# Expert rows loaded whole into three rooms, one comparison for both one-hots, sample rows left in PSUM

## The chip, the cores and the metric

One core of a Trainium2 chip runs the whole program. The metric is the device time of one execution in microseconds, lower is better. PE is TensorE, DVE VectorE, ACT ScalarE, POOL GpSimd and SP SyncE.

## What is computed

One decoder layer for a prompt group of 256 tokens and a sample group of 64 tokens: a mixer (state-space scan and short convolution), attention over 256 memory tokens, and PEER, a layer of 16384 single-neuron experts. The change lies in PEER. Its core, cut:

```
q = (xt @ wq).reshape(T, PEER_HEADS, 2, PEER_HALF)
s = einsum('thid,hikd->thik', q, sub_keys)
s1, i1 = top_k(s[:, :, 0], 16);  s2, i2 = top_k(s[:, :, 1], 16)
comb = s1[..., :, None] + s2[..., None, :]
sf, pos = top_k(comb, 16)            # 16 of 256 pairs in each of 8 heads
eid = i1 * 128 + i2 at pos;  g = softmax(sf)
act = gelu(einsum('td,tkd->tk', x, u[eid]))
out = einsum('tk,tkd->td', g * act, v[eid])
```

So every token takes 128 of the 16384 experts, each a row of 2048 numbers in `u` and one in `v` (128 MB each, as float32). All arithmetic is float32; matmuls run in a rounded format, so each operand is split into a high and a low part and each product takes three matmuls.

## The kernel before, in words

**Prompt tokens** are computed densely: for each of 128 blocks ("rows" in this text) of 128 experts the products of all 256 prompt tokens with all 128 experts are taken, and a gate matrix is laid over them that is zero where a token did not choose an expert. **Sample tokens** are gathered: for each of 64 places, 128 rows of `u` (1 MB) are fetched by an indirect transfer.

*Expert rows* (`u_unit(i, q)`, one call for a quarter q of row i, 512 units in all). Even quarters order half a row, 128 experts x 1024 columns, by four transfers into one 128x1024 tile `xt` (L1719, each to 32 partitions, in pieces of 256 numbers, 1 KB). DVE transposes 32x32 blocks (L1729, `tt`), ACT takes the high part (L1736, `H`), POOL or, when the planner finds POOL late, DVE the low part (L1739, L1742, `L`), and PE adds 12 matmuls to the row's sum `pu` (L1755 to L1757). After the fourth quarter ACT applies the Gelu (L1762, `at`) and SP stores the row of activations to DRAM (L1763).

*The order.* PE, ACT and DVE work in exactly the order in which the program issues instructions. The class `Stream` staggers each unit: its load is issued three units ahead of its first step, the second step one unit later, its matmuls six units after that. "Sides" (generators with a rate, so many steps for each unit) are woven in between: `choose` selects the experts, `sample_in` gathers and multiplies the sample rows, `gate_work` builds the gate matrices. SP and POOL queues keep their own in-order sequence of transfers.

*Rooms.* Weights, expert rows and value rows all take tiles of 128x1024 in turn from one ring of four (`wtile`, WB = 4).

*Sample products* (`sample_in`). The sample rows of x lie in SBUF (`XNAT`, copied from PSUM at L1488). For each place one DVE instruction multiplies the gathered 128x2048 tile `gu` with it and sums (L1612), and a second one reads the accumulator.

*Gates* (`one_hots`, `gates`). For four tokens at a time two one-hot matrices are made from the two key numbers of each choice (the key indices `n128p` lie in PSUM); the first is scaled by the gate. Normally DVE makes them, four comparisons with scaling of 128x128 (L1637) and one of 128x512 (L1645); when the planner finds ACT early enough, ACT makes the first kind (L1632, L1633). PE multiplies the two (L1661, `pgate`), ACT copies the result (L1674 to SBUF, L1671 to a tile that goes to DRAM). The tokens are in three parts, of 124, 76 and 56; the third part is kept in DRAM (`g2_d`) and read back in the value stage.

*Value stage* (`v_unit`). For each row the stored activations come back (L1844), POOL multiplies them by the three gate parts (L1852), ACT and DVE split the products and the value rows (L204, L205, `vt`), PE adds into eight PSUM banks, while sample values are gathered and added on DVE (L1805).

PSUM has eight banks, all handed out as tiles of 128x512 from one pool (`ps`).

## Time and profile before

| | us |
|---|---|
| median of the runs shown (3423.12, 3436.35, 3428.07) | 3428.07 |
| the profiled execution's own time | 3432.44 |
| its span, first to last instruction | 3430.7 |
| PE busy | 3212.5 |
| DVE busy | 2468.6 |
| ACT busy | 1580.3 |
| POOL busy | 1501.0 |

The expert rows' matmuls begin at 1721.8 us and end at about 2690; the value stage follows. A busy time is the union of an engine's instructions; the granted clock of PE is a share of its full 2.4 GHz, averaged over a stretch in which it is at one of its two levels, 1.2 and 2.4 GHz; the DMA share is the mean busy share of 16 engines.

### The profile page before, as it was taken

What the parts mean: (1) busy time and instruction counts of PE and PEld (TensorE: products, weight loads), DVE (VectorE), ACT (ScalarE), POOL (GpSimd) and SP (SyncE); (2) the same over time, 40 slices, a digit from 0 to 9 for tenths busy, and PEclk for the clock granted to TensorE, in tenths of its full rate; (3) what the DMA queues carried; (4) which work ended last, traced back from release to release, by engine and by line L of the source; (5) the groups of instructions that cost most, each with busy time, mean ns of one, the idle gap of its engine ahead of it and who ended that gap; (6) DMA issues with size and microseconds to landing.
All of it is one profiled execution on the core that took longest, in us unless ns stands there. A gap on an engine that the chain in (4) does not pass through costs nothing.

```text
span 3430.7 us, 60141 instructions
## 1 busy us (share of the span) xinstructions
PE 3212.5 (94%) x21357; PEld 3011.9 (88%) x21357; DVE 2468.6 (72%) x4393; ACT 1580.3 (46%) x3063; POOL 1501.0 (44%) x1555
## 2 busy tenths in 40 slices
PE   6999999999999998899999778888889999999997
PEld 6999999999999998799999778888889888878876
DVE  4556766666574577866777878898878588878875
ACT  4545543333553455554454344443334444444444
POOL 0001111111100002311288788887787677766753
PEclk8999999999999999999999999999999999999998
DMA  8664556555654587866887888999997999988986
GB/s 201 198 189 144 158 164 187 161 166 147 205 156 149 170 205 196 226 211 173 208 200 192 231 235 231 242 257 249 256 274 187 290 336 319 332 310 314 321 296 212
DMA packets 534922, 763.22 MB, mean 222 GB/s; under 512 B 46655, under 2 KB 447575, under 8 KB 525492
## 3 DMA queue, kind: packets, MB, share of 16 engines
q1 hardware_dynamic: 480060, 550.95, 56.2%
q0 software_dynamic: 54560, 208.44, 19.4%
q8 instruction: 167, 2.74, 0.3%
q14 instruction: 135, 1.11, 0.1%
HBM read 709.15 MB, written 49.80 MB: 221 GB/s over the span
## 4 chain that ended last, share of the span: by engine, by line
DMA 22%; PE 10%; issue 6%; DVE 6%; POOL 4%; SPq 2%; ACT 2%; DVEq 0%; POOLq 0%; ACTq 0%
DMA xt<-in_peer_u_dram 10%; DMA at<-act_d 6%; DMA gv<-in_peer_v_dram,EV 3%; PE pu L1757 2%; POOL L L1739 2%; PE pu L1755 2%; PE pu L1756 2%; DVE L L205 2%; DMA vt<-in_peer_v_dram 2%; POOL at L1852 2%; SPq L1719 2%; DVE tt L1729 1%; DVE slot L1805 1%; DMA act_d<-at 1%; DVE gu L1612 1%
## 5 line engine op out<-in xcount | busy, mean ns | idle before, releaser
L205 DVE TENSOR_TENSOR L<-W,H 128x512 fp32r<-128x512 f32 (+1 forms) x808 | 544.7, 701 | 291.9 <-ACT H L204 285.4
L1739 POOL TENSOR_TENSOR L<-tt,H 128x512 fp32r<-128x512 f32 x486 | 686.4, 1443 | 111.3 <-ACT H L1736 96.3
L1757 PE MATMUL pu<-XP,L 128*128 128x256 f32 x2048 | 599.9, 293 | 82.9 <-POOL L L1739 82.8
L204 ACT ACTIVATE H<-W 128x512 fp32r<-128x512 f32 (+1 forms) x808 | 476.0, 620 | 350.5 <-PE pg L287 241.8
L1755 PE MATMUL pu<-XP,H 128*128 128x256 f32 x2048 | 598.9, 292 | 18.7 <-ACT H L1736 12.4
L286 PE MATMUL pg<-AH,H 128*128 128x320 f32 (+1 forms) x1872 | 587.1, 314 | 3.9 <-ACT H L204 3.9
L1756 PE MATMUL pu<-XP,H 128*128 128x256 f32 x2048 | 590.3, 288 | 0.0
L288 PE MATMUL pg<-AH,L 128*128 128x320 f32 (+1 forms) x1872 | 578.7, 309 | 0.5 <-DVE L L205 0.5
L287 PE MATMUL pg<-AL,H 128*128 128x320 f32 (+1 forms) x1872 | 578.2, 309 | 0.0
L1736 ACT ACTIVATE H<-tt 128x512 fp32r<-128x512 f32 x512 | 316.6, 627 | 484.4 <-DVE tt L1729 411.2
L1757 PEld LDWEIGHTS pu<-XP,L 128*128 128x128 f32 x2048 | 404.3, 197 | 97.7 <-POOL L L1739 97.6
L1729 DVE STREAM_TRANSPOSE tt<-xt 128x512 f32<-128x512 f32 x512 | 341.3, 692 | 175.7 <-DMA xt<-in_peer_u_dram 155.3
L1755 PEld LDWEIGHTS pu<-XP,H 128*128 128x128 f32 x2048 | 405.2, 198 | 23.2 <-ACT H L1736 15.6
L1898 PE MATMUL acc<-L,wt 128*128 128x512 f32 x1024 | 402.5, 393 | 17.0 <-DVE L L205 16.5
L1756 PEld LDWEIGHTS pu<-XP,H 128*128 128x128 f32 x2048 | 404.4, 197 | 0.0
L1897 PE MATMUL acc<-H,wt 128*128 128x512 f32 x1024 | 400.4, 391 | 1.7 <-ACT H L204 1.7
L1899 PE MATMUL acc<-H,wt 128*128 128x512 f32 x1024 | 400.5, 391 | 0.0
L205 DVE TENSOR_TENSOR L<-vt,H 128x512 fp32r<-128x512 f32 x512 | 370.5, 763 | 36.6 <-ACT H L204 30.7
L286 PEld LDWEIGHTS pg<-AH,H 128*128 128x128 f32 (+1 forms) x1872 | 350.3, 187 | 9.0 <-ACT H L204 4.9
L204 ACT ACTIVATE H<-vt 128x512 fp32r<-128x512 f32 x512 | 292.1, 621 | 141.1 <-DMA vt<-in_peer_v_dram 91.8
L287 PEld LDWEIGHTS pg<-AL,H 128*128 128x128 f32 (+1 forms) x1872 | 350.4, 187 | 2.2
L288 PEld LDWEIGHTS pg<-AH,L 128*128 128x128 f32 (+1 forms) x1872 | 350.1, 187 | 1.9 <-DVE L L205 1.3
(491 smaller groups left out, 6157.6 us busy)
## 6 DMA issues: line engine op xcount, KB each, us to landing
xt<-in_peer_u_dram SPq DMA_DIRECT2D x1024, 128.0 KB
vt<-in_peer_v_dram SPq DMA_DIRECT2D x256, 512.0 KB
W<-in_w_in_dram SPq DMA_DIRECT2D x176, 512.0 KB
W<-in_w_out_dram SPq DMA_DIRECT2D x64, 512.0 KB
W<-in_w_mem_k_dram SPq DMA_DIRECT2D x32, 512.0 KB
W<-in_w_mem_v_dram SPq DMA_DIRECT2D x32, 512.0 KB
W<-in_w_mem_q_dram SPq DMA_DIRECT2D x32, 512.0 KB
kv<-in_cache_mem_k_dram SPq DMA_DIRECT2D x128, 128.0 KB
```

Of the source, the lines that this page charges most:

```text
L204: S.activation(h, src, AF.Copy)
L205: V.tensor_tensor(l, src, h.bitcast(F32), ALU.subtract)
L286: PE.matmul(out, hv[:, j, c0:c1], ah[:, k, 0:n], start=st, stop=False)
L287: PE.matmul(out, hv[:, j, c0:c1], al[:, k, 0:n], start=False, stop=False)
L288: PE.matmul(out, lv[:, j, c0:c1], ah[:, k, 0:n], start=False, stop=sp)
L1739: G.tensor_tensor(l, src, h.bitcast(F32), ALU.subtract)
L1755: PE.matmul(pu[:, 0:TP], hv[:, j], PP["xp"][:, 0, k], start=k == 0, stop=False)
L1756: PE.matmul(pu[:, 0:TP], hv[:, j], PP["xp"][:, 1, k], start=False, stop=False)
L1757: PE.matmul(pu[:, 0:TP], lv[:, j], PP["xp"][:, 0, k], start=False, stop=k == KC - 1)
L1897: PE.matmul(out, th, h, start=i == 0, stop=False)
L1898: PE.matmul(out, th, l, start=False, stop=False)
L1899: PE.matmul(out, tl, h, start=False, stop=i == P - 1)
```

## The change

1. **Rooms.** The ring becomes one tile of four rooms that the program hands out and takes back itself (`wtile`, `wtile2`, `wfree`); a pair of neighbouring rooms holds a whole row of 128x2048. When the selection begins, a third pair is added (`more`, from the smaller gate matrix: the parts of the tokens are now 108, 76 and 72). In the value stage the six rooms serve as halves.
2. **Row transfers.** A row is ordered at its first quarter by four transfers, each to 32 partitions as before but in pieces of 512 numbers, 2 KB, in the order 0, 2, 1, 3 of the partition groups. The layout of the prompt tokens' x in `xp` follows (columns 512 b + 128 ... for group b).
3. **Sample rows** stay in the four PSUM banks in which the transposition left them; each sample product becomes four instructions of 128x512 with accumulators in `DOT[..., 4]`, and one reduction at the end. As long as they live, no transposed quarter goes to PSUM.
4. **One-hots.** Both keys of four tokens in one DVE comparison of 128x1024; ACT scales the first by the gates, four times 128x128.
5. **Gates in DRAM.** The third part, now 72 tokens, is read back in four pieces into two halves of the slot in turn; the sample sum `ACC` moves to `GT`.
6. Small: `row`, `xs` and the key rows get tiles of their own or one room after the other.

The diff, cut:

```diff
-NG0, NG1 = 124, 76
+NG0, NG1 = 108, 76
 NG2 = TP - NG0 - NG1
-NGA = 8
+NGA = 6
...
-    def wtile(name="W"):
-        return wp.tile([P, 1024], F32, tag="W", bufs=WB, name=name)
+    wroom = cst.tile([P, 1024 * WB], F32, name="W")
+    rooms = [[wroom[:, 1024 * r:1024 * r + 1024], None, 0] for r in range(WB)]
+    turn = count(1)
+
+    def wtile(beside=None):
+
+        r = min((r for r in range(len(rooms)) if rooms[r][1] is None),
+                key=lambda r: (rooms[r ^ 1][1] is not beside, rooms[r][2]))
+        rooms[r][1] = rooms[r][0]
+        return rooms[r][0]
+
+    def wtile2():
+
+        r = min((r for r in range(0, len(rooms), 2) if rooms[r][1] is rooms[r + 1][1] is None),
+                key=lambda r: max(rooms[r][2], rooms[r + 1][2]))
+        w = (wroom if r < WB else more)[:, 1024 * (r % WB):1024 * (r % WB) + 2048]
+        rooms[r][1] = rooms[r + 1][1] = w
+        return w
...
     def key_rows():
-        kys = []
         for i in range(2):
-            kys.append(wtile("ky").rearrange("p (h c) -> p h c", c=P))
-            nc.sync.dma_start(kys[i], sub_keys[0, 4 * i:4 * i + 4].rearrange("h i k c -> k (h i) c"))
-        yield from wait(2)
...
+            ky = wtile()
+            nc.sync.dma_start(ky.rearrange("p (h c) -> p h c", c=P),
+                              sub_keys[0, 4 * i:4 * i + 4].rearrange("h i k c -> k (h i) c"))
+            yield from wait(2)
...
+        more = pL.tile([P, 2048], F32, name="W")
+        rooms.extend([more[:, 1024 * r:1024 * r + 1024], None, 0] for r in range(2))
...
-            S.activation(XNAT[:, 512 * q:512 * q + 512], pt, AF.Copy)
+            XNAT.append(pt)
...
                 gt = tiles.pop(j - AIN)
-                V.tensor_tensor_reduce(gt, gt, XNAT, 1.0, 0.0, ALU.mult, ALU.add, DOT[:, j - AIN:j - AIN + 1])
-                run("dve", 2.25, arrived.pop(j - AIN))
-            yield 1
-        S.activation(WS, DOT, AF.Gelu)
+                for q in range(4):
+                    part = gt[:, 512 * q:512 * q + 512]
+                    V.tensor_tensor_reduce(part, part, XNAT[q], 1.0, 0.0, ALU.mult, ALU.add, DOT[:, j - AIN, q:q + 1])
+                run("dve", 2.9, arrived.pop(j - AIN))
+            yield 1
+        XNAT.clear()
+        V.tensor_reduce(WS, DOT, AX.X, ALU.add)
+        S.activation(WS, WS, AF.Gelu)
...
-        by_act = [clock["act"] + A_MORE + 2 * i < clock["dve"] for i in range(2)]
+        at = run("dve", 1.3)
+        V.tensor_tensor(ov, PP["n128"].unsqueeze(1).unsqueeze(1).broadcast_to([P, 2, 4, P]),
+                        GT[:, 0:2, t0:t0 + 4].unsqueeze(3).broadcast_to([P, 2, 4, P]), ALU.is_equal)
+        yield ov, at
         for j in range(4):
...
-                at = run("dve", 0.26)
-                V.tensor_scalar(ov[:, 0, j], n128p, key(0), key(3), op0=ALU.is_equal, op1=ALU.mult)
...
+            S.activation(ov[:, 0, j], ov[:, 0, j], AF.Copy, scale=GT[:, 3, t0 + j:t0 + j + 1])
+            at = run("act", 0.3, at)
+            if j != 1:
+                yield ov, at
...
-            if q % 2 == 0:
-                xt = wtile("xt")
-                c0 = 512 * q
-                for b in range(4):
+            if q == 0:
+                xt = box["x", i] = wtile2()
+                for b in (0, 2, 1, 3):
                     nc.sync.dma_start(xt[32 * b:32 * b + 32].rearrange("p (a d) -> p a d", a=4),
-                                      U2[i * P:(i + 1) * P, c0 + 256 * b:c0 + 256 * b + 256].rearrange("(a p) d -> p a d", p=32))
-                box["x", i, q // 2] = xt
+                                      U2[i * P:(i + 1) * P, 512 * b:512 * b + 512].rearrange("(a p) d -> p a d", p=32))
...
-            tt = two("tt") if box["pool", n] else ps("tt")
+
+            tt = two("tt") if box["pool", n] or XNAT else ps("tt")
...
-        ACC = slot[:, 0:1024]
-        G2 = slot[:, 1024:1024 + P * NG2].rearrange("p (n x) -> p n x", x=4 * P)
+        ACC = GT.rearrange("p j t -> p (j t)")
+        G2 = [slot[:, 4096 * r:4096 * r + 32 * NG2].rearrange("p (n x) -> p n x", x=P) for r in range(2)]
...
-            if q == 1 and i in (4, 6, 8, 10):
-                r = i // 2 - 2
-                c0 = max(P * r, 4 * NGA)
-                nc.sync.dma_start(G2[:, :, c0:P * r + P], g2_d[:, :, c0:P * r + P])
+
+            if q == 1 and i in (2, 4, 36, 68):
+                r = (2, 4, 36, 68).index(i)
+                c0 = 4 * NGA if r == 0 else 0
+                nc.sync.dma_start(G2[r % 2][:, :, c0:], g2_d[:, :, P * r + c0:P * r + P])
```

How the instructions move, as the built programs have them. First SP, in the middle of the expert rows, with what each order waits for (DMAHW0 to 7 are the eight counters of its transfers, taken in turn, so each waits for the transfer eight places earlier; DVE for the room, Activation for the Gelu). Before, from one activation store to the next:

```order
L1763 DMA act_d<-at 128x256 [waits DMAHW3_49,Activation_49]
L1719 DMA xt<-in_peer_u_dram 32x4x256 [waits DMAHW4_49,DVE_49]
L1719 DMA xt<-in_peer_u_dram 32x4x256 [waits DMAHW5_49]
L1719 DMA xt<-in_peer_u_dram 32x4x256 [waits DMAHW6_49]
L1719 DMA xt<-in_peer_u_dram 32x4x256 [waits DMAHW7_49]
L1719 DMA xt<-in_peer_u_dram 32x4x256 [waits DMAHW0_49,DVE_49]
L1719 DMA xt<-in_peer_u_dram 32x4x256 [waits DMAHW1_49]
L1719 DMA xt<-in_peer_u_dram 32x4x256 [waits DMAHW2_49]
L1719 DMA xt<-in_peer_u_dram 32x4x256 [waits DMAHW3_49]
L1763 DMA act_d<-at 128x256 [waits DMAHW4_49,Activation_49]
```

and of the change:

```order
L1788 DMA act_d<-at 128x256 [waits DMAHW4_49,Activation_49]
L1743 DMA W<-in_peer_u_dram 32x4x512 [waits DMAHW5_49,DVE_49]
L1743 DMA W<-in_peer_u_dram 32x4x512 [waits DMAHW6_49]
L1743 DMA W<-in_peer_u_dram 32x4x512 [waits DMAHW7_49]
L1743 DMA W<-in_peer_u_dram 32x4x512 [waits DMAHW0_49]
L1788 DMA act_d<-at 128x256 [waits DMAHW1_49,Activation_49]
```

Between the stores of rows i and i+1 stood the second half of row i+3 and the first half of row i+4; now the whole of row i+4 stands there, in half as many orders. (Before the first store 28 orders, three and a half rows, stood there; now 16, four rows.)

Second DVE, where gathers and gates run beside the rows. Before:

```order
L1637 TENSOR_SCALAR oh<-n128p,GT 128x128
L1729 STREAM_TRANSPOSE tt<-xt 128x512
L1637 TENSOR_SCALAR oh<-n128p,GT 128x128
L1729 STREAM_TRANSPOSE tt<-xt 128x512
L1612 ISA gu,DOT<-gu,XNAT 128x2048
L1612 ISA DOT 128x1
L1729 STREAM_TRANSPOSE tt<-xt 128x512
L1637 TENSOR_SCALAR oh<-n128p,GT 128x128
L1645 TENSOR_TENSOR oh<-n128p,GT 128x512
```

and of the change:

```order
L1665 TENSOR_TENSOR oh<-n128p,GT 128x1024
L1752 STREAM_TRANSPOSE tt<-W 128x512 x3
L1648 ISA gu,DOT<-gu,pxn 128x512
L1648 ISA DOT 128x1
L1648 ISA gu,DOT<-gu,pxn 128x512
L1648 ISA DOT 128x1
L1648 ISA gu,DOT<-gu,pxn 128x512
L1648 ISA DOT 128x1
L1648 ISA gu,DOT<-gu,pxn 128x512
L1648 ISA DOT 128x1
L1752 STREAM_TRANSPOSE tt<-W 128x512 x2
```

The comparisons that lay between single transpositions are one instruction; a sample product is four pairs in a row at the same place.

Third ACT, where the gates are built. Before:

```order
L1762 ACTIVATE at<-pu 128x256
L1736 ACTIVATE H<-tt 128x512 x2
L1674 ACTIVATE G_23732<-pgate 128x128x4
L1736 ACTIVATE H<-tt 128x512 x2
L1762 ACTIVATE at<-pu 128x256
```

and of the change:

```order
L1787 ACTIVATE at<-pu 128x256
L1669 ACTIVATE oh<-oh,GT 128x128 x2
L1699 ACTIVATE G_23174<-pgate 128x128x4
L1761 ACTIVATE H<-tt 128x512
L1669 ACTIVATE oh<-oh,GT 128x128
L1761 ACTIVATE H<-tt 128x512 x3
L1787 ACTIVATE at<-pu 128x256
```

Between one row's Gelu and the next, four scalings have joined the high parts and the copy of a gate tile. DVE's program holds 27 low parts of its own (26 before); 24 of them read a quarter in SBUF.

## Rows read from the trace of the kernel before

**Rows 1.** The page's head: span, busy time of each engine.

```profile
span 3430.7 us, 60141 instructions
PE 3212.5 (94%) x21357; PEld 3011.9 (88%) x21357; DVE 2468.6 (72%) x4393; ACT 1580.3 (46%) x3063; POOL 1501.0 (44%) x1555
```

**Rows 2.** Busy time by stretches; after the engines the granted clock, DMA share, GB/s.

```profile
core 0: us, PE busy (x) PEld busy (x) DVE busy (x) ACT busy (x) POOL busy (x), PEclk, DMA share, GB/s
0.00:1711.00 1711.00, 1645.10 (x11513) 1592.58 (x11514) 1087.25 (x2219) 810.48 (x1578) 238.33 (x464) 0.99 0.63 181
...
1760.00:1810.00 50.00, 50.00 (x419) 50.00 (x418) 41.47 (x137) 24.96 (x47) 47.66 (x38) 1.00 0.91 211
1810.00:2610.00 800.00, 681.41 (x5278) 661.59 (x5277) 656.13 (x961) 335.08 (x650) 657.11 (x459) 0.95 0.91 241
2610.00:2660.00 50.00, 50.00 (x429) 50.00 (x428) 47.34 (x111) 25.04 (x48) 32.60 (x26) 1.00 0.62 153
...
2691.00:3431.00 740.00, 706.52 (x3072) 578.78 (x3072) 592.15 (x807) 346.24 (x670) 466.63 (x519) 0.98 0.89 307
```

**Rows 3.** Groups in 1810 to 2610: count, busy us, mean ns, idle before.

```profile
L1739 POOL TENSOR_TENSOR L<-tt,H 128x512 fp32r<-128x512 f32 x383 | 555.3, 1479 | 76.9 <-ACT H L1736 65.2 <-PE pu L1756 3.6 <-DVE tt L1729 3.2
...
L1729 DVE STREAM_TRANSPOSE tt<-xt 128x512 f32<-128x512 f32 x408 | 272.8, 693 | 135.9 <-DMA xt<-in_peer_u_dram 118.7 <-POOL L L1739 15.0 <-issue 1.8
...
L1612 DVE CUSTOM_DVE_ANT_0 gu<-gu,XNAT 128x2048 f32<-128x2048 f32 x64 | 232.6, 3635 | 0.0
...
L1637 DVE TENSOR_SCALAR oh<-n128p,GT 128x128 f32<-128x128 f32 x152 | 56.6, 375 | 0.0
...
L1645 DVE TENSOR_TENSOR oh<-n128p,GT 128x512 f32<-128x512 f32 x47 | 31.7, 674 | 0.0
L1633 ACT ACTIVATE oh<-oh,GT 128x128 f32<-128x128 f32 x40 | 19.8, 495 | 1.3
...
L1742 DVE TENSOR_TENSOR L<-tt,H 128x512 fp32r<-128x512 f32 x26 | 17.4, 669 | 5.1 <-ACT H L1736 5.1
...
L1612 DVE DVE_READ_ACCUMULATOR2_ANT DOT<- 128x1 f32 x64 | 5.0, 78 | 0.0
```

**Rows 4.** Who waited for whom in 1810 to 2610: us in total, times, longest.

```profile
ACT H L1736 <- DVE tt L1729: 366.9, 186, 8.1
DVE tt L1729 <- DMA xt<-in_peer_u_dram: 118.7, 65, 6.2
...
PE pu L1757 <- POOL L L1739: 82.8, 70, 6.3
POOL L L1739 <- ACT H L1736: 65.2, 55, 5.9
```

**Rows 5.** The chain of waits through 1810 to 2610, shares by line.

```profile
by line: DMA xt<-in_peer_u_dram 40.3%; issue 14.1%; POOL L L1739 8.9%; SPq L1719 6.7%; DVE tt L1729 5.4%; PE pu L1757 3.9%; PE pu L1756 3.4%; PE pu L1755 3.4%; DVE gu L1612 2.6%; ACT H L1736 2.0%; DMA act_d<-at 1.5%; POOL gu L1607 1.0%; DVE
```

**Rows 6.** What SP's queue waited for in 1810 to 2610: total, times, longest.

```profile
SPq L1763 <- ACT at L1762: 117.8, 68, 8.0
SPq L1719 <- DMA xt<-in_peer_u_dram: 101.4, 104, 4.1
```

**Rows 7.** The sample products L1612: ns least, median, most.

```profile
L1612 DVE CUSTOM_DVE_ANT_0 gu<-gu,XNAT x64: 2248/2794/8392, 1905.4 to 2593.4; 128x2048 f32<-128x2048 f32 x64
```

**Rows 8.** The group of POOL's subtractions in 1710 to 1850.

```profile
L1739 POOL TENSOR_TENSOR L<-tt,H 128x512 fp32r<-128x512 f32 x86 | 109.6, 1312 | 19.3 <-ACT H L1736 18.0 <-PE pu L1756 1.1
```

**Rows 9.** Short stretches: weights in 2 KB, in 1 KB; then three inside G.

```profile
1500.00:1540.00 40.00, 40.00 (x275) 40.00 (x274) 25.31 (x46) 20.27 (x39) 0.00 (x0) 1.00 0.58 192
1560.00:1600.00 40.00, 40.00 (x275) 39.83 (x274) 24.36 (x41) 17.84 (x34) 0.24 (x1) 1.00 0.42 132
...
1960.00:2010.00 50.00, 34.99 (x254) 33.84 (x253) 38.78 (x49) 17.61 (x32) 47.02 (x27) 0.86 0.77 206
2110.00:2160.00 50.00, 36.70 (x266) 35.72 (x265) 46.39 (x52) 25.17 (x55) 41.01 (x26) 0.83 0.72 187
2510.00:2560.00 50.00, 41.95 (x332) 40.12 (x331) 37.39 (x40) 18.11 (x34) 43.76 (x32) 1.00 1.03 277
```

More of the change, by code (lines that the diff above doesn't have):

```diff
@@ L184, in step, with wfree @@
     GAIN = cst.tile([P, 96], F32, name="GAIN")
-    def wtile(name="W"):
-        return wp.tile([P, 1024], F32, tag="W", bufs=WB, name=name)
+    wroom = cst.tile([P, 1024 * WB], F32, name="W")
[12 more added lines that the diff above has]
+        return w
+    def wfree(w):
+        for r in rooms:
+            if r[1] is w:
+                r[1:] = None, next(turn)
+    more = None
     def high():
@@ L252, in load @@
                 if kq in (0, 2) and w0 is not None:
-                    box["w"] = w0[kq // 2]
+                    box["room", kq + 1] = w0[kq // 2]
+                    box["w"] = w0[kq // 2].rearrange("p (k n) -> p k n", n=ncol)
                 elif kq % 2 == 0:
-                    w = wtile()
+                    w = box["room", kq + 1] = wtile(box["room", kq - 1] if kq % 4 else None)
                     wv = w[:, 0:4 * ncol].rearrange("p (k n) -> p k n", n=ncol)
@@ L267, in prep @@
                 split(hv, lv, box.pop(("w", kq))[:, 2 * q:2 * q + 2])
+                if q == 1:
+                    wfree(box.pop(("room", kq)))
                 box[kq] = (hv, lv)
@@ L361, in step @@
     mem = [tokens() for _ in range(2)]
-    w0 = [wtile().rearrange("p (k n) -> p k n", n=256) for _ in range(2)]
+    w0 = [wtile()]
+    w0.append(wtile(w0[0]))
     for i in range(2):
@@ L618, in put_columns @@
         for q in range(nchunk // 8):
-            row = wtile("row")[0:ncol]
+            row = pS.tile([P, 1024], F32, tag="row", bufs=1, name="row")[0:ncol]
             for g in range(2):
@@ L993, in load @@
                 if k % 2 == 0:
[L994 removed]
+                    box["room", k + 1] = wtile()
+                    w = box["room", k + 1].rearrange("p (k n) -> p k n", n=512)
                     nc.sync.dma_start(w, w2d[k * P:(k + 2) * P, 512 * c:512 * c + 512].rearrange("(k p) n -> p k n", p=P))
@@ L1006, in prep @@
                     split(h, l, src)
+                if k % 2:
+                    wfree(box.pop(("room", k)))
                 box[k] = h, l
@@ L1338, in open_p @@
         strm.side(norm_p(), 1)
-        strm.side(key_rows(), 0.5)
+        strm.side(key_rows(), 0.75)
         PP["normed"] = strm.side(normed(), 0.4)
@@ L1349, in key_rows @@
     def key_rows():
[L1350 removed]
         for i in range(2):
[L1352 to L1360 removed]
+            ky = wtile()
+            nc.sync.dma_start(ky.rearrange("p (h c) -> p h c", c=P),
+                              sub_keys[0, 4 * i:4 * i + 4].rearrange("h i k c -> k (h i) c"))
+            yield from wait(2)
+            for q in range(2):
+                pt = ps("pky")
+                for j in range(4):
+                    transpose(pt[:, j * P:(j + 1) * P], ky[:, 512 * q + P * j:512 * q + P * j + P])
+                S.activation(PP["KY"][:, 8 * i + 4 * q:8 * i + 4 * q + 4], pt.rearrange("p (j k) -> p j k", k=P), AF.Copy)
+                yield 1
+            wfree(ky)
         done.add(("ky",))
@@ L1386, in normed @@
                 if q % 2 == 0:
-                    xs = wtile("xs")[0:n]
+                    xs = pp.tile([P, 1024], F32, tag="xs", bufs=1, name="xs")[0:n]
                 pt = ps("pxs")
@@ L1457, in step @@
         gemm(w_peer_q[0], 256 * c, 256, BH, BL, T, lambda m, pt, c=c: evac_p(m, pt, c))
-    pL = pT = GT = EID = EV = GS = DOT = WS = XNAT = None
+    pL = pT = GT = EID = EV = GS = DOT = WS = None
+    XNAT = []
     def choice_in():
-        nonlocal pL, pT, GT, EID, EV, GS, DOT, WS, XNAT
+        nonlocal more, pL, pT, GT, EID, EV, GS, DOT, WS
         drain(PP["normed"])
@@ L1576, in choose @@
             if tb < 2:
+                yield from wait(2)
                 pt = ps("pgt")
```

47 lines of the change are left out of this document (14 added, 33 removed).

## The prediction, before the change was run

> **What bounds the kernel now.** I read the page first: the span is 3430.7 us and PE is busy for 3212.5 us of it [rows 1], so at most some 218 us are to be had from waits. The profiled execution's own time is 3432.44 us, 1.74 above its span; the median of the runs shown is 3428.07, so 4.37 us come off a time that is summed against the profiled execution. A difference under 0.5%, 17 us, can't be told from no change here.
>
> Then the busy time by stretches [rows 2]. PE is busy without a gap at 1760 to 1810 and at 2610 to 2660, at a granted clock of 1.00 (2.4 GHz). Between them, from 1810 to 2610 (stretch G), it is busy for 681.4 of 800 us at a mean granted clock of 0.95: 118.6 us of idle time. Of the two long stretches around it the first has 65.9 us of idle time in 1711 and the last, the expert values, 33.5 in 740. G is where the selection, the 64 gathers and most of the gate one-hots run beside the expert rows, and every row of the change that costs or saves more than a few us lies in it. 408 quarters of a row (a quarter is one transposition L1729, so G holds 102 of the 128 rows) are worked there [rows 3].
>
> Then the waits in G, from PE backwards [rows 4]. PE waits for POOL's low parts (82.8 us), POOL for ACT's high parts (65.2), ACT for DVE's transpositions (366.9), DVE for the expert rows in flight (118.7). The chain of waits in G names those transfers with 40.3% of the stretch, and the matmuls with some 11% [rows 5]. So the rows come late, and it is not one engine that is full: DVE 656, POOL 657, ACT 335 of 800 us, the DMA engines 0.91 [rows 2]. SyncE, which orders the transfers, itself waits 117.8 us for an activation behind which the next rows are queued, and 101.4 us for a transfer of eight places earlier to land [rows 6].
>
> **The change part by part.**
>
> *Sample products on DVE.* Before, 64 products of 128x2048 take 232.6 us and their 64 accumulator reads 5.0, 237.6 together [rows 3]. After, there are 256 of 128x512 with one operand in PSUM and 256 reads. The nearest row is the subtraction of the same size with a PSUM source, L1742, 669 ns; with a read of 78 ns [rows 3] one costs 747 ns, and 256 cost 191.2 us: 46.4 us less. Bounds: a quarter of the shortest old product, 2248/4 = 562 ns [rows 7], gives 163.8 us (73.8 less); a quarter of the mean, 3635/4 = 909 ns [rows 3], gives 252.7 us (15.1 more). The old product lies between 2248 and 8392 ns with the same operands [rows 7], and POOL's subtraction took 1312 ns before the first product [rows 8] and 1479 in G [rows 3]: each lengthens the other. I take 747 ns for that reason, and give POOL the difference back, 383 x (1479 - 1312) = 64 us of its busy time; at worst nothing.
>
> The Trainium skill, SBUF — State Buffer, section "SBUF: two separate sides", states for this that a VectorE instruction with two SBUF inputs shuts GpSimd's reads out for its whole length and the other way round, and that one with a single SBUF input does not. By it the new products run undisturbed, and DVE's gain is the 46 us or more; by the mean alone it would be a loss of 15. The spread of 2248 to 8392 ns agrees with the rule. It also speaks against one edit: while the products run, a quarter that DVE subtracts itself now has both inputs in SBUF.
>
> That last edit concerns 24 of 27 such quarters (26 before, all from PSUM). From 669 ns each they can grow by what a POOL subtraction lasts, 1479 ns [rows 3]: 0 to 35 us on DVE. I take 10.
>
> *One-hots on DVE and ACT.* Four tokens cost DVE up to 4 x 375 + 674 = 2174 ns. G holds 152 of the first kind and 47 of the second, 56.6 + 31.7 = 88.3 us [rows 3]. Now it is one comparison of 128x1024. The slope between 512 and 2048 elements, (2248 - 674)/1536 = 1.02 ns an element [rows 3, 7], makes it 674 + 524 = 1198 ns; 47 of them 56.3 us, 32 less (bounds: 2 x 674 = 1348 ns gives 25 less; 674 + 375 = 1049 ns gives 39 less). ACT takes over 256 scalings of 128x128; at the 495 ns of its nearest row [rows 3] they are 127 us at most, for 188 of them (47 groups) in G 93. In G it is busy for 335 of 800 us [rows 2], which covers this as long as nobody waits for a place in its queue; if that cover is gone, see the third rival.
>
> DVE's work in G so falls from 656 by 46 - 10 + 32 = 68 to 588 us, POOL's from 657 to 593.
>
> *Transfers.* 1024 orders of 128 KB in pieces of 1 KB become 512 of 256 KB in pieces of 2 KB. SyncE gives half as many orders, and eight that are under way are 2 MB instead of 1. By the rows of its order, what follows an activation's store was the second half of the row three ahead and the first of the row four ahead; now it is the whole row four ahead, so half a row more has been ordered at the same point. Three rooms hold 3 MB where four held 2. None of this removes the wait for the activation; it is a later row that is queued behind it. The last activations and the value loads behind them keep their order.
>
> The price of a piece isn't in the trace. Weights in pieces of 1 KB run at 132 GB/s with a share of 0.42, 314 GB/s if the engines were full; those in pieces of 2 KB at 192 and 0.58, 331 [rows 9]: 5% less time per byte. Expert rows alone, in 1 KB, run at 211 and 0.91, 232 full; at 153 and 0.62, 247 [rows 2]. With 247, the 408 quarters of 256 KB, 107 MB, hold 433 of the 728 us (0.91 of 800) that the engines are busy in G. Bounds: nothing saved; or the rows reach the weights' 331, 107/0.331 = 323 us, 110 less. I take a tenth, 43 us: twice the weights' ratio, because more is under way and neighbours in the queue go to different halves of the partitions, and far from 110, because each transfer still lands in 32 partitions, as the slow rows do. That leaves 685 us.
>
> *What G then lasts.* The transfers set it: before, 728 us of work took 800, a share of 0.91. At the same share 685 us take 753; at 0.94, with a deeper reserve, 729. The other floors are lower: PE's 681 us at 0.95 of the clock, between 647 and 681; DVE 588; POOL 593. I take 745 us: **55 us less**. Half of the 118.6 us of idle time goes; what is late next is still the row, then POOL's subtraction.
>
> *The rest.* The value stage gets six rooms instead of four, 1 MB more of gates to write and read back (3.4 us of transfers at its 307 GB/s [rows 2]) and gives its gates to POOL in parts of 108, 76 and 72 instead of 124, 76 and 56. With 33.5 us of idle time in it I take 0, between 10 less and 10 more. The first 1711 us hold the same transfers in the same order in the same four rooms; the key rows take one room after the other instead of two at once: 0, at most 3 either way. Four copies of the sample rows (now read where the transposition left them) and a reduction of 256 values are under 3 us, beside other work.
>
> Sum: 3432.4 - 55 = 3377 for a profiled execution, **3373 us** as a median.
>
> **The rivals.**
>
> *A: the rows can't come faster.* If 32 partitions are the limit, the pieces' size saves nothing. For it: the rows alone reach 0.91 at only 211 GB/s [rows 2], while weights over all partitions reach 314 [rows 9]. Against it: 277 GB/s ran in one 50 us stretch with the gathers [rows 9]. Then only the places gain where DVE was late and the transfers were not full, such as 1960 to 2010 and 2110 to 2160, shares of 0.77 and 0.72, 28 us of PE idle time together [rows 9]; of that some 17: 3411. The Trainium skill, SBUF — State Buffer, "Door 1: The DMA port swizzle", has this as a rule: 32 partitions reach 8 of 16 ports, about 218 GB/s at most, and two transfers to different halves at once bring 6% over one. By it G would keep its 728 us but for those 6% of 433, 26 us; the 211 GB/s agree, and no run here shows the order's part.
>
> *B: the rows cease to be the limit.* With 323 us for the rows G needs 618 us of transfers, 657 at 0.94, and PE's floor is at 647 to 681: some 680, 120 less, 3308. For it: all idle time lies in G. Against it: nothing shows 331 GB/s into 32 partitions.
>
> *C: PSUM takes it back.* While the products run, four of eight banks hold the sample rows and one the key indices; three are left for the rows' sums and the gates, where transpositions and sums had seven. In the built program 27 of 64 gate tiles take a bank whose sum ended only two to four quarters before, and 29 sums one that a gate tile left four to seven quarters before. Such a bank is free when ACT has read it, and in ACT's order that read stands behind the high parts of five further quarters. ACT waits for a transposition 186 times, 366.9 us in G [rows 4], 1.97 us each. If each of the 56 takings meets one such wait, PE stands still for 110 us; less the gain, 55 more than before: 3483. It decides from (55 + 17)/1.97, some 37 takings, on. Against it: two quarters are 2.9 us at PE's pace of 1.43 us (12 matmuls at 419 in 50 us [rows 2]), and with rows on time ACT is ahead.
>
> *D: no change that can be seen*, the gains of G given back in part by DVE's double-input quarters and by ACT's longer queue: 3424.
>
> **How the numbers follow.** Forecast 0.53, A 0.17, B 0.10, C 0.12, D 0.08. A lies at the 17 us bound, half of it either side. Faster: 0.53 + 0.10 + 0.08 = 0.71; within 0.5%: 0.09 + 0.08 = 0.17; slower: C, 0.12. The range takes in the forecast with its bounds, A, D and the nearer part of B: 3322 to 3430. Left out are C and the far end of B.
>
> **What would show it.** Right: in G (found again as the stretch between two gapless ones) idle time of PE near 60 us; DVE's waits for the rows well under 118 us; SyncE's wait for a landing under 50; products near 0.67 us with little spread and POOL's subtraction near 1.3 us. A: DMA share at 0.95 or more with the same GB/s and DVE still waiting for rows. C: PE waiting at a gate tile or at a row's first matmul for ACT's reads (at<-pu, G<-pgate), tens of times. The forecast is wrong if the stretch shortens by under 25 or by over 90 us, or if the value stage moves by over 10.

## The result and the profile after

The changed kernel takes 3388.19 us (median of 4 runs, 3382.60 to 3394.76), the kernel before beside it 3432.21 (3423.12 to 3446.70): a ratio of 0.987, 95% interval 0.984 to 0.990, 44 us less. 3373 was forecast, in a range of 3322 to 3430. The profiled execution is the longest of the four: 3394.76 us, span 3393.0.

The page's head, beside [rows 1]:

```profile
span 3393.0 us, 59499 instructions
PE 3210.2 (95%) x21357; PEld 3016.0 (89%) x21357; DVE 2373.0 (70%) x4563; ACT 1609.9 (47%) x3235; POOL 1421.2 (42%) x1554
```

DVE works 96 us less, POOL 80 less, ACT 30 more, PE nearly the same: what went is PE's idle time. The busy time by stretches, columns as in [rows 2]:

```profile
1760.00:1810.00 50.00, 50.00 (x419) 50.00 (x418) 43.61 (x147) 25.38 (x48) 45.62 (x37) 1.00 0.87 214
1810.00:2580.00 770.00, 686.52 (x5389) 669.31 (x5388) 587.76 (x1224) 365.77 (x782) 596.53 (x466) 0.96 0.93 254
2580.00:2630.00 50.00, 50.00 (x429) 50.00 (x428) 31.57 (x39) 39.06 (x103) 32.24 (x26) 1.00 0.68 164
```

G, between two gapless stretches, is now 1810 to 2580 us and holds 83.5 us of PE's idle time, where it held 118.6 [rows 2]. From the first expert-row matmul to the first value matmul it is 928.5 us (1731.8 to 2660.3), before 969.6 (1721.8 to 2691.4): 41 less. This is the row stage. The value stage behind it is 7 shorter. The row stage begins 10 later in this execution; in the ten experiments that keep the changed kernel's first part it begins between 1723.0 and 1728.0 (before: 1721.8), so most of the 10 is this execution's own.

The waits in the stretch, beside [rows 4] (total us, times, longest), all engines first, then the rest of PE's:

```profile
ACT H L1761 <- DVE tt L1752: 325.9, 171, 8.7
DVE tt L1752 <- DMA W<-in_peer_u_dram: 143.6, 51, 7.7
POOL L L1764 <- ACT H L1761: 128.8, 96, 5.9
PE pu L1782 <- POOL L L1764: 31.3, 35, 4.1
...
PE pu L1780 <- ACT H L1761: 12.2, 9, 2.9
PE pgate L1686 <- ACT at L1787: 10.2, 4, 4.5
PE pu L1780 <- ACT G L1699: 7.1, 3, 3.1
PE pu L1780 <- ACT g L1696: 6.1, 3, 2.7
PE pgate L1686 <- ACT g L1696: 5.1, 4, 3.0
PE pgate L1686 <- ACT G L1699: 3.7, 2, 2.5
PE pgt L220 <- ACT at L1787: 3.6, 1, 3.6
```

PE's wait for POOL fell from 82.8 to 31.3 us. New are waits until ACT has read a PSUM bank: the last six rows, and one of 0.8 us more, make 36.6 us in 18 waits. Two waits in the selection are gone that PE had before in 1810 to 2610 us:

```profile
PE pgt L197 <- DVE GA L1574: 15.9, 2, 8.3
```

There PE stood until DVE had the gates of a group of tokens ready (`GA`), which PE then transposes (`pgt`). The change has a line for this that its cut diff leaves out: `yield from wait(2)` lets the program put other work between the two. No run undoes that line alone.

VectorE's wait for rows has not fallen: 143.6 us where it was 118.7, in fewer waits but longer ones. VectorE works 68 us less in a stretch that is 30 us shorter, so it stands idle for longer in any case; this wait by itself doesn't tell how late the rows are. SyncE's waits, beside [rows 6]:

```profile
SPq L1788 <- ACT at L1787: 329.1, 81, 9.0
SPq L1788 <- ACT oh L1669: 66.4, 16, 8.2
SPq L1697 <- ACT g L1696: 41.3, 18, 5.1
SPq L1788 <- DMA W<-in_peer_u_dram: 24.4, 24, 4.3
SPq L1743 <- DMA W<-in_peer_u_dram: 11.8, 14, 1.8
SPq L1743 <- DVE tt L1752: 8.5, 22, 0.9
```

SyncE hardly waits for landings (101.4 us before) or rooms. It stands at the activation's store for over half the stretch, with the next row's order behind it. The groups, beside [rows 3, 8], and the products alone (ns min/median/max), beside [rows 7]:

```profile
L1648 DVE CUSTOM_DVE_ANT_0 gu<-gu,pxn 128x512 f32<-128x512 f32 x256 | 158.8, 674 | 0.0
L1665 DVE TENSOR_TENSOR oh<-n128p,GT 128x1024 f32<-128x1024 f32 x51 | 60.6, 1187 | 0.0
L1767 DVE TENSOR_TENSOR L<-tt,H 128x512 fp32r<-128x512 f32 x27 | 38.4, 1423 | 1.4 <-ACT H L1761 1.0 <-issue 0.3
L1648 DVE DVE_READ_ACCUMULATOR2_ANT DOT<- 128x1 f32 x256 | 20.9, 82 | 0.0
...
L1764 POOL TENSOR_TENSOR L<-tt,H 128x512 fp32r<-128x512 f32 x390 | 505.9, 1323 | 142.1 <-ACT H L1761 128.8 <-PE pu L1782 5.8 <-issue 1.8
```

```profile
L1648 DVE CUSTOM_DVE_ANT_0 gu<-gu,pxn x256: 641/681/687, 1906.9 to 2558.4; 128x512 f32<-128x512 f32 x128
```

### The profile page after: what moved, and what is told of

The parts are those of the page before. It is cut to its first block, busy times and chain, and to the rows that moved or that the text cites. A ratio compares the mean times of both kernels' runs of the same rounds, so it can differ in the third digit from the quotient of the medians.

```text
span 3393.0 us, 59499 instructions
## 1 busy us (share of the span) xinstructions
PE 3210.2 (95%) x21357; PEld 3016.0 (89%) x21357; DVE 2373.0 (70%) x4563; ACT 1609.9 (47%) x3235; POOL 1421.2 (42%) x1554
## 4 chain that ended last, share of the span: by engine, by line
DMA 18%; PE 14%; DVE 8%; issue 5%; POOL 3%; ACT 2%; SPq 1%; DVEq 0%; ACTq 0%; POOLq 0%
DMA W<-in_peer_u_dram 8%; DMA at<-act_d 6%; PE pu L1782 3%; PE pu L1780 3%; PE pu L1781 2%; DMA gv<-in_peer_v_dram,EV 2%; DVE tt L1752 2%; DVE L L228 2%; POOL at L1880 2%; DVE gu L1648 1%; PE acc L1929 1%; PE acc L1930 1%; PE acc L1928 1%; POOL L L1764 1%; SPq L1743 1%
## 5 line engine op out<-in xcount | busy, mean ns | idle before, releaser
L228 DVE TENSOR_TENSOR L<-W,H 128x512 fp32r<-128x512 f32 x1320 | 913.1, 724 | 324.2 <-ACT H L227 307.0
L227 ACT ACTIVATE H<-W 128x512 fp32r<-128x512 f32 x1320 | 762.2, 620 | 409.3 <-PE pg L313 246.0
L1764 POOL TENSOR_TENSOR L<-tt,H 128x512 fp32r<-128x512 f32 x485 | 626.3, 1318 | 171.5 <-ACT H L1761 150.6
L1782 PE MATMUL pu<-XP,L 128*128 128x256 f32 x2048 | 593.5, 290 | 32.9 <-POOL L L1764 31.3
L1752 DVE STREAM_TRANSPOSE tt<-W 128x512 f32<-128x512 f32 x512 | 332.0, 686 | 213.1 <-DMA W<-in_peer_u_dram 161.8
L1782 PEld LDWEIGHTS pu<-XP,L 128*128 128x128 f32 x2048 | 401.1, 196 | 42.5 <-POOL L L1764 40.7
L1880 POOL TENSOR_TENSOR at<-at,G 128x108 f32<-128x108 f32 (+1 forms) x256 | 209.3, 837 | 219.0 <-DMA at<-act_d 199.5
L1929 PEld LDWEIGHTS acc<-L,wt 128*128 128x128 f32 x1024 | 192.9, 188 | 58.5 <-DVE L L228 18.2
```

The costliest lines, as they stand in the source:

```text
L227: S.activation(h, src, AF.Copy)
L228: V.tensor_tensor(l, src, h.bitcast(F32), ALU.subtract)
L1764: G.tensor_tensor(l, src, h.bitcast(F32), ALU.subtract)
L1782: PE.matmul(pu[:, 0:TP], lv[:, j], PP["xp"][:, 0, k], start=False, stop=k == KC - 1)
L1929: PE.matmul(out, th, l, start=False, stop=False)
```

## Experiments

Twelve kernels, each beside the kernel before. The ratio is to the kernel before, with its 95% interval; the kernel before had a median of 3432 to 3437 us beside them, so a difference of under 5 us from the changed kernel tells nothing. "Longer" and "shorter" are against the changed kernel's 3388 us. The last column is the row stage in the profiled execution, from the first expert-row matmul to the first value matmul; it is 969.6 us in the kernel before.

| run | edit | us | ratio | row stage, us |
|---|---|---|---|---|
| changed kernel | | 3388 | 0.987 (0.984 to 0.990) | 928.5 |
| e1 | its order 0, 1, 2, 3 | 3415 | 0.994 (0.993 to 0.996) | 953.4 |
| e2 | 1 KB pieces | 3392 | 0.989 (0.986 to 0.991) | 926.6 |
| e3 | products against SBUF | 3414 | 0.993 (0.991 to 0.995) | 949.3 |
| e4 | old one-hots | 3390 | 0.986 (0.983 to 0.989) | 931.6 |
| e5 | transfers over 128 partitions | 4105 | 1.195 (1.192 to 1.197) | 1640.6 |
| e7 | two rooms | 3450 | 1.004 (1.003 to 1.006) | 978.0 |
| e8 | sums share banks | 3423 | 0.997 (0.995 to 0.999) | 970.5 |
| e9 | stores on ACT's queue | 3399 | 0.990 (0.987 to 0.993) | 927.5 |
| e10 | half rows | 3415 | 0.994 (0.993 to 0.996) | 959.3 |
| e12 | store one row later | 3370 | 0.982 (0.979 to 0.986) | 904.9 |
| e6 | before, order 0, 2, 1, 3 | 3415 | 0.995 (0.993 to 0.997) | 952.2 |
| e11 | before, that order and PSUM products | 3398 | 0.990 (0.987 to 0.994) | 941.0 |

**e1, the order alone.**

```diff
-                for b in (0, 2, 1, 3):
+                for b in range(4):
```

> The changed kernel with one line undone: each expert row's four transfers go out as 0, 1, 2, 3 and not as 0, 2, 1, 3. Theory one (the rows come sooner because the pieces are 2 KB and a row is whole, the order is worth nothing): 3388 us within 6 us of the changed kernel, TensorE's idle time between 1810 and 2580 us stays about 84 us. Rival (two neighbouring groups of 32 partitions fill through the same engines, and the swapped order is what spreads them): 15 to 40 us longer, 3403 to 3428 us, with DVE's waits for the rows in that stretch above 143.6 us.

3415 us, 27 longer: the rival. The stretch 1810 to 2580 and its wait for rows:

```profile
1810.00:2580.00 770.00, 677.59 (x5225) 658.76 (x5225) 567.31 (x1203) 350.32 (x742) 576.31 (x451) 0.94 0.97 249
```

```profile
DVE tt L1752 <- DMA W<-in_peer_u_dram: 175.2, 56, 8.9
```

Fewer bytes a second (249 for 254 GB/s) at a higher share (0.97 for 0.93): per byte the engines are busy 6% longer (0.97/249 against 0.93/254).

**e6, the order in the kernel before.** The same line there, the other way round.

> The kernel before with one line of the change: the four transfers of each half row go out as 0, 2, 1, 3 and not as 0, 1, 2, 3; 1 KB pieces, two double rooms, products and one-hots as before. Theory port (the order raises the rate into SBUF wherever rows are late): 10 to 25 us shorter than the kernel before, 3407 to 3422 us beside 3432. Rival (the order pays only once rows are whole and three are held, or once the products no longer hold GpSimd): within 6 us of 3432 us.

3415 us, some 20 less than the kernel before beside it (22 by the medians, 18 by the ratio). The same 770 us of this kernel, and of the kernel before:

```profile
1810.00:2580.00 770.00, 661.88 (x5166) 642.73 (x5164) 651.62 (x936) 327.70 (x637) 645.42 (x447) 0.95 0.86 247
```

```profile
1810.00:2580.00 770.00, 652.78 (x5042) 633.37 (x5041) 632.13 (x921) 320.61 (x623) 627.92 (x439) 0.95 0.91 242
```

0.86/247 against 0.91/242: 7% less engine time per byte, with 1 KB pieces and half rows. The order works by itself. The Trainium skill, SBUF — State Buffer, "Door 1: The DMA port swizzle", puts partitions 0 to 63 and 64 to 127 on different ports, and its section "Can I just issue two DMAs to hit both halves?" gives two transfers to different halves at once only 6% over one. Both pairs agree with the direction. That the sizes agree too is not shown: the 6 and 7% are of all bytes in the stretch, of which the rows are little more than half in the changed kernel (417 quarters of 256 KB, 109 of 196 MB), and e2 moves the share by 5% with no effect on the time.

**e2, the pieces alone.**

```diff
-                for b in (0, 2, 1, 3):
-                    nc.sync.dma_start(xt[32 * b:32 * b + 32].rearrange("p (a d) -> p a d", a=4),
-                                      U2[i * P:(i + 1) * P, 512 * b:512 * b + 512].rearrange("(a p) d -> p a d", p=32))
+                for h in range(2):
+                    for b in (0, 2, 1, 3):
+                        c0 = 512 * b + 256 * h
+                        nc.sync.dma_start(xt[32 * b:32 * b + 32].rearrange("p (a d) -> p a d", a=4)[:, :, 256 * h:256 * h + 256],
+                                          U2[i * P:(i + 1) * P, c0:c0 + 256].rearrange("(a p) d -> p a d", p=32))
```

> The changed kernel with each row's transfers halved: eight of 128 KB with 1 KB pieces in place of four of 256 KB with 2 KB pieces; rooms, order of the groups, products and one-hots stay as changed. Theory one (the piece size is worth the tenth that the prediction put on it, 43 us of the row transfers' 433 us in G): 25 to 45 us longer, 3413 to 3433 us, and the DMA share of the stretch at 1.00. Rival port (a row fills 32 partitions at a time at a rate that the piece size does not touch): within 6 us of 3388 us. [...]

3392 us: no difference that can be told. The pieces are worth nothing, and so is that more bytes are under way, since eight orders are half as many bytes here:

```profile
1810.00:2580.00 770.00, 688.56 (x5390) 672.69 (x5389) 584.81 (x1205) 369.29 (x793) 592.72 (x463) 0.95 0.88 254
```

The same 254 GB/s and the same work of PE, at a lower share. The share is not a fill: probably packets that wait in line count in it, and with orders of 128 KB instead of 256 KB fewer do. SyncE waits 121.3 us for landings again, and that costs nothing.

**e3, the products alone.** The sample rows are copied to SBUF as before, one product of 2048 columns a step.

```diff
-            XNAT.append(pt)
+            S.activation(XN["sb"][:, 512 * q:512 * q + 512], pt, AF.Copy)
...
-                for q in range(4):
-                    part = gt[:, 512 * q:512 * q + 512]
-                    V.tensor_tensor_reduce(part, part, XNAT[q], 1.0, 0.0, ALU.mult, ALU.add, DOT[:, j - AIN, q:q + 1])
+                V.tensor_tensor_reduce(gt, gt, XN["sb"], 1.0, 0.0, ALU.mult, ALU.add, DOT[:, j - AIN:j - AIN + 1])
```

> The changed kernel with the sample rows back in SBUF: one product of 2048 columns per sample step with both operands in SBUF, and four more PSUM banks free; rooms, transfers and one-hots stay as changed. Theory one (products that read PSUM relieve DVE and GpSimd): VectorE's products go from 179.7 us in 1810 to 2580 us to about 238 us, GpSimd's subtractions from 1.32 to about 1.5 us, and the kernel is 20 to 40 us longer, 3408 to 3428 us. Rival C (three banks take it back): the waits of matmuls on ScalarE's reads, about 36 us of TensorE's time, vanish and the kernel is 10 to 25 us shorter, 3363 to 3378 us. If both hold in equal measure, within 8 us of 3388 us, with the bank waits under 10 us and VectorE's and GpSimd's waits up by as much.

3414 us, 26 longer: theory one, though the banks' waits went as rival C has it. The product, POOL's subtraction, and PE's only waits of size:

```profile
L1647 DVE CUSTOM_DVE_ANT_0 gu<-gu,XNAT 128x2048 f32<-128x2048 f32 x64 | 247.6, 3869 | 0.1
...
L1761 POOL TENSOR_TENSOR L<-tt,H 128x512 fp32r<-128x512 f32 x370 | 547.9, 1510 | 63.3 <-ACT H L1758 54.3 <-issue 2.8 <-PE pu L1779 2.1
```

```profile
PE pu L1779 <- POOL L L1761: 90.6, 84, 7.0
PE pu L1777 <- ACT H L1758: 11.8, 14, 2.7
```

No wait for a bank is left, and PE's wait for POOL is back at 90.6 us. So the products against PSUM take away 59 us of waits for POOL (90.6 to 31.3) and bring 36.6 of waits for banks; what is left, 23, is about the 26 measured. VectorE's wait for rows is shorter here, 85.5 us, in a slower kernel.

**e4, the one-hots alone.** `one_hots` and the copy to GT as before.

```diff
-        at = run("dve", 1.3)
-        V.tensor_tensor(ov, PP["n128"].unsqueeze(1).unsqueeze(1).broadcast_to([P, 2, 4, P]),
-                        GT[:, 0:2, t0:t0 + 4].unsqueeze(3).broadcast_to([P, 2, 4, P]), ALU.is_equal)
+        by_act = [clock["act"] + A_MORE + 2 * i < clock["dve"] for i in range(2)]
...
```

> The changed kernel with the old one-hots: per four tokens one multiply-compare a token for the first key and one comparison for the second, some of both put on ScalarE, in place of one comparison of 1187 ns and four gate scalings of 392 ns. Theory one (VectorE's time matters only where a row has landed, and rows are late): VectorE works some 30 us more in 1810 to 2580 us, of which a third reaches TensorE, 5 to 15 us longer, 3393 to 3403 us. Rival (the scaling on ScalarE delays the high parts, and the old form is as good): within 5 us of 3388 us or up to 10 us shorter.

3390 us: DVE is busy 610.8 us in the stretch instead of 587.8, and no part of that can be told in the time. The one-hots are worth nothing.

**e7, the third room alone.**

```diff
-        more = pL.tile([P, 2048], F32, name="W")
-        rooms.extend([more[:, 1024 * r:1024 * r + 1024], None, 0] for r in range(2))
```

> The changed kernel without the third room: the rows whole in two rooms of 1 MB, the value stage in four rooms of 512 KB; all else as changed. Theory one (the third room lets a row be ordered while two are unread): 15 to 35 us longer, 3403 to 3423 us, with SyncE waiting for VectorE's transpositions before its row orders instead of for the activation. Rival (SyncE stands at the activation's store anyway, 329 us in 1810 to 2580 us, so that the third room is free long before the order comes): within 6 us of 3388 us.

3450 us, 61 longer: theory one's sign at twice its size, and 0.4% slower than the kernel before. Of the 61 some 50 lie in the row stage; the value stage, back in four rooms, has the rest. SyncE's two longest waits:

```profile
SPq L1741 <- DVE tt L1750: 219.2, 81, 8.3
SPq L1786 <- ACT at L1785: 207.9, 67, 7.0
```

A room of 1 MB comes free only when the whole row in it is transposed, and SyncE now stands before its row orders until then. Whole rows need the third room; without it they cost more than order and products give.

**e10, half rows in the six rooms.**

```diff
-            if q == 0:
-                xt = box["x", i] = wtile2()
+            if q % 2 == 0:
+                xt = box["x", i, q // 2] = wtile()
+                c0 = 512 * q
...
```

> The changed kernel with half rows again: each half row in one of the six rooms of 512 KB, four transfers of 128 KB in the order 0, 2, 1, 3, ordered half by half as in the kernel before; products, one-hots and the rest as changed. Theory one (what pays is the order, the products and half as much again of room; that a row is whole is worth nothing or costs, since its first transposition waits for all of it): 5 to 30 us shorter, 3358 to 3383 us. Rival (whole rows pay because a whole row is ordered at one place of SyncE's queue, ahead of the next store): 10 to 30 us longer, 3398 to 3418 us.

3415 us, 27 longer: the rival. VectorE's wait for rows:

```profile
DVE tt L1753 <- DMA W<-in_peer_u_dram: 182.9, 73, 7.5
```

It is not the pieces, since e2 has the same 1 KB in whole rows. What is left is that a row's second half is ordered two quarters later in the program, behind one store more, and into a room of its own; these were not taken apart.

**e11, order and products in the kernel before.** The edits of e6, and of e3 the other way round.

> The kernel before with two parts of the change: the order 0, 2, 1, 3, and the sample products in four pieces against PSUM; half rows in four rooms of 512 KB and the old one-hots stay. Theory one (these two parts are the whole gain, whole rows with the third room come to nothing together): the order's 20 and the products' 26 us add up, 3380 to 3396 us. Rival (the parts need the third room: with less in reserve the bank waits of three PSUM banks meet late rows): 3400 to 3430 us.

3398 us, between the two ranges: 34 of the 44 us come from these two parts, and the order's 20 leave 14 to the products there. All the rest of the change together, whole rows, third room, one-hots and the selection's `wait(2)`, is worth the other 10. PE's two waits at `pgt` are still there in e11, 12.4 us, so the `wait(2)` may be most of it; that is not shown. That e10, with two half rooms more, the new one-hots and the `wait(2)`, takes 17 us longer than e11 is not explained: the two also differ in how the tokens are cut (108, 76, 72 against 124, 76, 56) and in where the key rows lie.

**e5, transfers over all partitions.**

```diff
-                for b in (0, 2, 1, 3):
-                    nc.sync.dma_start(xt[32 * b:32 * b + 32].rearrange("p (a d) -> p a d", a=4),
-                                      U2[i * P:(i + 1) * P, 512 * b:512 * b + 512].rearrange("(a p) d -> p a d", p=32))
+                for a in range(4):
+                    nc.sync.dma_start(xt[:, 512 * a:512 * a + 512],
+                                      U2[i * P + 32 * a:i * P + 32 * a + 32].rearrange("p (b d) -> b p d", b=4))
```

> The changed kernel with each row's four transfers cut the other way: one transfer takes 32 experts whole and fills a 2 KB piece in each of the 128 partitions, in place of 128 experts' quarter into 32 partitions; same bytes, pieces, number of orders and same place of every value in SBUF. Theory port (how fast a row lands depends on which partitions the transfers under way fill; that is why the order 0, 2, 1, 3 is worth 27 us): the rows land sooner still, VectorE's waits for rows in 1810 to 2580 us fall from 143.6 to under 90 us and the kernel is 15 to 45 us shorter, 3343 to 3373 us. Rival (the order helped only by when the first half of a row is there, not by the rate): within 8 us of 3388 us. A third way: sixteen engines share each transfer in another way and the rate falls, over 3400 us.

4105 us: the third way, far beyond its bound. The queue's share between 1760 and 1900 us, and a row order on SyncE (ns min/median/max):

```profile
q1 hardware_dynamic: 8628, 15.17, 28.8%
```

```profile
L1743 SPq DMA_DIRECT2D W<-in_peer_u_dram x512: 522/2381/9178, 1701.6 to 3333.2; - x171
```

The share stands near a quarter while everything waits for rows, at 109 GB/s, and an order takes SyncE 2381 ns in the median instead of 430 in the changed kernel. A quarter fits four of sixteen engines, as many as the source has outer blocks here; the trace doesn't list the engines apart, so that is argued. What an even spread over the partitions would give stays open.

**e8, two sums in one bank.**

```diff
             if q == 0:
-                box["p"] = ps("pu")
+                if i % 2 == 0:
+                    box["pp"] = ps("pu")
+                box["p"] = box["pp"][:, TP * (i % 2):TP * (i % 2) + TP]
```

> The changed kernel with two expert rows' sums in the two halves of one PSUM bank, so that the sums take 64 banks in place of 128; all else as changed. Theory C (some 36 us of TensorE's idle time in 1810 to 2580 us are waits until ScalarE has read a bank): the waits of gate tiles and first matmuls of a row on ScalarE fall to under 12 us, half of what goes is met by a later wait for a row, 8 to 20 us shorter, 3368 to 3380 us. Rival (rows are what is late, and a bank wait only stands in for a wait for a row): within 6 us of 3388 us, the waits on rows up by what the bank waits lose.

3423 us, 35 longer, and no test of theory C. Nearly all of the gate tiles' waits did go, but:

```profile
PE pu L1782 <- ACT at L1789: 107.3, 49, 11.6
```

The sums of two rows are one tile here, and the odd row's first matmul (L1782 in this kernel) waits until ACT has read the even row's half. Separate halves weren't tried.

**e9, the stores on ACT's queue.**

```diff
-                nc.sync.dma_start(act_d[:, i], at)
+                nc.scalar.dma_start(act_d[:, i], at)
...
-                    nc.sync.dma_start(g2_d[:, (t - t0) // 4], g2)
+                    nc.scalar.dma_start(g2_d[:, (t - t0) // 4], g2)
```

> The changed kernel with the stores of the activations and of the g2 gates issued from ScalarE's own queue behind the instruction that makes them, so that SyncE's queue holds only the row orders in this stretch; all else as changed. Theory one (SyncE stands 329 + 66 + 41 us of 770 at those stores with the next row queued behind them, and the third room lies empty meanwhile): row orders go out when a room is free, VectorE's waits for rows in 1810 to 2580 us fall from 143.6 to under 100 us, and the kernel is 15 to 35 us shorter, 3353 to 3373 us. Rival (the transfers are at 0.93 of the DMA engines there, an earlier order only queues longer): within 8 us of 3388 us, with SyncE's waits moved to VectorE's transpositions and to landings. A third way: each store costs ScalarE its issue, 146 times some 50 to 400 ns, up to 58 us of ScalarE's time, and rows' high parts wait for it: up to 15 us longer.

3399 us, its interval overlapping the changed kernel's, and its row stage the same within 1 us: not theory one. The 11 us more by the medians are allowed by the third way, but don't show in the row stage. The wait only changed its name:

```profile
SPq L1743 <- DMA act_d<-at: 433.3, 91, 10.6
```

In the built program a row's order waits until the transfer eight places earlier has landed, whichever queue that went out on, and there are only four orders to a row. So each row still waits for a store.

**e12, the store one row later.** On SyncE's queue row i+4 now stands ahead of the store of row i.

```diff
-                nc.sync.dma_start(act_d[:, i], at)
+                for r, a in ((i - 1, box.get("at")), (i, at))[0 if i else 1:1 if i < P - 1 else 2]:
+                    nc.sync.dma_start(act_d[:, r], a)
+                box["at"] = at
```

> The changed kernel with the store of each row's activations written one row later in the program, so that on SyncE's queue row i+4 stands ahead of the store of row i instead of behind it; ScalarE's queue, the rooms, and everything else as changed. Theory one (row orders come late because the store's wait for the activation stands ahead of them; with the stores on ScalarE's queue the wait only moved to their landing, since an order waits for the one eight places earlier): SyncE's waits at the store fall from 395 to under 250 us of the 770, VectorE's waits for rows from 143.6 to under 110 us, and the kernel is 10 to 30 us shorter, 3358 to 3378 us. Rival (with DMA shares of 0.93 to 1.00 an earlier order only queues longer, as the run with the stores on ScalarE's queue already suggests): within 8 us of 3388 us.

3370 us, theory one in all its numbers: 1.8% faster than the kernel before, and 18 us shorter than the changed kernel by the medians. Their intervals overlap a little (0.979 to 0.986 and 0.984 to 0.990), but the row stage is clear: 904.9 us, where the changed kernel, e2, e4 and e9 lie between 926.6 and 931.6.

```profile
1810.00:2580.00 770.00, 706.03 (x5639) 690.96 (x5639) 605.16 (x1239) 388.75 (x842) 613.66 (x481) 0.97 0.96 260
```

```profile
DVE tt L1752 <- DMA W<-in_peer_u_dram: 102.2, 39, 5.9
```

```profile
SPq L1743 <- DVE tt L1752: 127.5, 51, 7.3
SPq L1743 <- DMA W<-in_peer_u_dram: 104.4, 113, 3.9
SPq L1697 <- ACT g L1696: 79.8, 17, 8.3
SPq L1789 <- DMA W<-in_peer_u_dram: 62.4, 47, 4.5
SPq L1789 <- ACT at L1787: 55.7, 23, 7.0
SPq L1789 <- ACT oh L1669: 36.4, 13, 6.4
```

PE's idle time falls from 83.5 to 64.0 us, the waits for ACT at the store of activations from 395.5 to 92.1 (those at the gates' store L1697 rise from 41.3 to 79.8). Now SyncE waits most for rooms and landings. Of the sizes that the prediction gave the change's waits, this edit comes near PE's 60 us and brings VectorE's wait under 118; the landings, 104.4, stay far above its 50.

## Why the prediction was right, and where it was not

- **What bounds the kernel.** Right in the main: the gain lies in G, 41 us of it in the row stage. But the rows were not the only limit there, as the next points show.
- **The sum.** It put all 55 us down to the transfers, and took DVE and POOL only as floors that lie lower. Here it is incomplete: undoing the products alone costs 26 us (e3), and beside the order they give some 14 (e11), through PE's waits for POOL. PE's 15.9 us of waits in the selection, which are gone, stand in no term either. That 44 came near 55 is in part luck: parts that the sum left out stood in for one that it took too large.
- **Transfers, 433 us shorter by a tenth.** This is the step that failed. It laid the tenth on the pieces, on more under way and on the two halves of the partitions together. The first two together give nothing (e2). The order alone gives 27 or some 20 us of time (e1, e6). By the prediction's own measure, share over rate, the engines' time per byte fell by 3% from the kernel before (0.91/241 to 0.93/254), which is 22 us of its 728 instead of 43; e2 shows how rough that measure is.
- **Sample products, 46.4 us less on DVE, 747 ns each.** Mechanism right, size a little low: the product is at 674 ns and the read at 82, but the reads fall together with the next product, so that all 256 hold DVE for 179.7 us, 702 ns each. The old ones took 237.6, so 58 are gone (the working had the new ones at 191). The products spread from 641 to 687 ns where the old form ran from 2248 to 8392 [rows 7] and in e3 from 2244 to 8899. POOL's subtraction is at 1323 ns, 1312 was taken. The rule of the Trainium skill, SBUF — State Buffer, "SBUF: two separate sides", that two SBUF inputs on VectorE shut out GpSimd's reads, agrees with both.
- **DVE's own low parts, 10 us more.** The direction was right, the size double: 27 took 1423 ns in the mean instead of 669, 20 us.
- **One-hots, 32 us less on DVE.** The length was right (1187 ns, 1198 taken); undone, DVE works 23 us more, and e4 shows no effect on the time.
- **"Half a row more has been ordered at the same point."** Right, but its worth is open. Without the third room the kernel loses 61 us (e7), without the whole row 27 (e10), yet the kernel that has neither lacks only 10 (e11). The working named the order behind the store and let it pass as "a later row"; in fact SyncE stands there nearly three times as long as before, and e12 shows that some 18 us hung on it.
- **G, 55 us less.** 41 came. Besides the transfers' term, rival C is a candidate for what is missing: 18 waits for banks of 2.03 us, 36.6 us, which the products bring (e3). Its price (1.97 us) was right; its count (56 takings) was three times too high. What the waits cost by themselves is not shown, since e8 was no test of it.
- **What would show it.** PE's idle time in G 83.5 (near 60 forecast): half wrong. Landings 11.8 and 24.4 us (under 50): right. VectorE's wait for rows 143.6 (well under 118): wrong, and a poor sign, since it grows when VectorE has less to do; PE's wait for POOL was the better one. The value stage moved by 7, under its bound of 10, and that need not be the change's: from its first to its last matmul it is 723.9 us before, 717.1 in the changed kernel and 717.4 in e6, which has the old form.

The parts don't add up: undone one at a time, order, products and third room cost 27 + 26 + 61 = 114 us, where together they gave 44. Whole rows in two rooms are a loss that the third room repays.

## What to carry to other kernels

When transfers are late, look first at what stands ahead of their orders on the issuing queue: a store that waits for its data holds up every load behind it, and putting it one round later can be worth more than larger pieces. Moving it to another queue didn't help here, where an order waits for the transfer eight places earlier. Send neighbouring transfers to different halves of the partitions. Undo a many-part change one part at a time, since the pieces and the one-hots did nothing here, and also add parts to the old kernel, since what one part costs when it is undone isn't what it gave.

## What was not expected of the hardware

- Four transfers of the same bytes, swapped in order, are worth 20 to 27 us, and the engines are busy 6 to 7% less per byte, with 1 KB and with 2 KB pieces alike.
- A higher DMA share is no proof of a fuller engine: 0.93 and 0.88 both moved 254 GB/s (e2).
- A transfer that covers all 128 partitions from a source of four outer blocks ran at a share of 0.29 and 109 GB/s, and its order held SyncE for 2381 ns in the median.
